# One cast and one subtraction per streamed weight tile instead of two of each

## The chip, the cores and the metric

The program runs on one core of a Trainium2 chip. The metric is the time of one execution on the device in microseconds (us), taken as the median of the runs; lower is better. Before the change the three runs took 1419.07, 1419.39 and 1425.46 us, so the median is 1419.39 us.

## The reference

The kernel computes one layer of a diffusion backbone for 256 latent tokens and 256 context tokens of width 2048, all in float32. Cut to what matters here:

```python
mod = silu(c) @ w_ada + b_ada                  # 2048 x 12288, six vectors
h  = rms_norm(x,   g_attn) * (1 + sc_a) + sh_a
hc = rms_norm(ctx, g_attn) * (1 + csc_a) + csh_a
q, k, v, ... = split(h @ w_in), split(hc @ w_in)   # 2048 x 4928
o = concat(neighbourhood(...), gqa(...), mla(...), diff(...))
x = x + gt_a * (o @ w_out)                     # 2048 x 2048
h = rms_norm(x, g_ffn) * (1 + sc_f) + sh_f
x = x + gt_f * ((silu(h @ wg) * (h @ wu)) @ wd)    # three of 2048 x 5632
return rms_norm(x, g_final)
```

Each weight matrix is read from DRAM once, a tile at a time.

## The kernel before, in words

TensorE multiplies in a rounded float32 form (F32R in the code). To keep the precision, every operand is split into a high part, which is the value cast to that form, and a low part, which is the value less the high part. A product is then three matmuls: high with high, high with low and low with high.

A streamed weight tile is 256 rows by 512 columns (320 or 256 in two places), that is two blocks k of 128 rows side by side in SBUF, `raw` [128, 2, 512]. Its way is always the same. SyncE (SP) issues one DMA of 512 KB into one of four `raw` buffers (`stream_raw`, L115). ScalarE (ACT) casts it into `whi`, one cast for each k (L127). VectorE (DVE) subtracts it into `wlo`, one subtraction for each k (L130). TensorE (PE) then runs the high products of both k (L150 and L151) and after them the low products (L153), in `mm3s`. `whi` and `wlo` have six buffers of [128, 512] each (`WB = 6`), enough for three weight tiles. A `raw` buffer comes free when the second subtraction has read it, and only then does SP issue the next DMA into it. The same four `raw` buffers also take the tiles of `w_ada` for the gate and FFN modulation vectors; those are multiplied and summed on DVE (`ada_block`, L335 on ACT for the first, L337 on DVE for the others), and they mingle with the weight tiles in two stretches of the run.

The stages in order of time are: tokens, normalisation and the first columns of the modulation (to about 60 us); the columns of `w_in` for the first two head groups, summed over five groups of K, with more of the modulation on TensorE (60 to 280); the other columns of `w_in` with the attention of the head groups in between (280 to 520); `w_out` (520 to 645); SwiGLU with `ffn_wg`, `ffn_wu` and `ffn_wd` (from 645), where `w_ada` tiles are still mixed in until about 820; and the final norm (from about 1400).

Two things set the order of the work. `Side` is a planner in the program's text: attention and modulation tasks are generators with costs in us, and `pump` traces their next stage between the weight tiles. What it decides does not depend on the split. Behind it the framework that builds the program lays the traced instructions out on each engine by the time at which it plans them to be ready, so the order on an engine is not quite that of the text; `tc.issue_after` (in `after`, with `newest`) pins a few instructions behind others. At run time each engine takes its instructions strictly in order.

Three more places keep split weights for longer, in pools of their own: `keep_w` (pool `rt`, `RT = 14` buffers, for the end of `w_out` and the first columns of `ffn_wg`), and the last columns of `ffn_wd` (pool `rt2`, 8 buffers). `stream_up` splits the small matrices of the latent attention, in one case as four blocks of 256 columns.

Of the kernel before, what the change touches and what calls it, by code (L numbers as in the profile page):

```python
# [10 lines left out]
F32 = mybir.dt.float32  # L11
F32R = mybir.dt.float32r
# [19 lines left out]
class Side:  # L32
    """Instructions traced in between the weight tiles of the main stream.

    A task is a generator that yields (time it takes of the tensor engine, time its
    results need) in us; its next stage is traced once the main stream has gone on
    for that long. Lanes are worked on independently, `width` tasks of a lane at once.
    """

# [48 lines left out]
def hybrid_dit_kernel(ctx: ExitStack, tc: tile.TileContext, a, out):  # L88
# [16 lines left out]

    # ------------------------------------------------------------ helpers
    def misc():
# [9 lines left out]

    WB = 6
    newest = {}

    def split(raw, n, keep=None):
        """hi and lo parts of raw [128, k, n], one pair per k"""
        out_ = []
        pool_, bufs = keep or (stream, WB)
        for k in range(raw.shape[1]):
            hi = pool_.tile([P, n], F32R, name="whi", tag="whi", bufs=bufs)
            act.copy(hi, raw[:, k])  # L127
            newest["act"] = nc.cur_bb.bb.instructions[-1]
            lo = pool_.tile([P, n], F32R, name="wlo", tag="wlo", bufs=bufs)
            dve.tensor_tensor(out=lo, in0=raw[:, k], in1=hi.bitcast(F32), op=ALU.subtract)  # L130
            newest["dve"] = nc.cur_bb.bb.instructions[-1]
            out_.append((hi, lo))
        return out_

# [4 lines left out]
    def after(*ins):  # L139
        """what the block traces on an engine of ins is issued behind them"""  # L140
        st = ExitStack()
        for i in ins:
            st.enter_context(tc.issue_after(i))
        return st

    def mm3s(jobs, w_left=False):
        """l @ r from their parts for each (bank, l, r, start, stop); the products with the
        low part of the weights come after all the others"""
        for dst, l, r, start, stop in jobs:
            pe.matmul(dst, lhsT=l[0], rhs=r[0], start=start, stop=False)  # L150
            pe.matmul(dst, lhsT=l[0 if w_left else 1], rhs=r[1 if w_left else 0], start=False, stop=False)  # L151
        for dst, l, r, start, stop in jobs:
            pe.matmul(dst, lhsT=l[1 if w_left else 0], rhs=r[0 if w_left else 1], start=False, stop=stop)  # L153
# [13 lines left out]

    # ------------------------------------------------------------ tokens and small vectors
    x_t = {}
# [43 lines left out]

    # ------------------------------------------------------------ normalised tokens, features on partitions
    xnT = [None] * 8
# [34 lines left out]
    def ada_pe(pr):  # L250
        """shift and scale of chunks 2 pr, 2 pr + 1 for both streams: column tile j of the
        tensor engine takes chunk j % 2 of the shift (j < 2) or the scale"""
        mv = misc()
        for k2 in range(0, KC, 2):
            raw = sb0.tile([P, 2, 2, 256], F32, name="araw", tag="araw", bufs=4)
            for kk in range(2):
                sp.dma_start(raw[:, kk], ada_two[:, k2 + kk, :, pr * 256:(pr + 1) * 256])
            for kk in range(2):
                kc = k2 + kk
                for j in range(4):  # L260
                    pe.matmul(mv[32 * j:32 * j + 32, :P], lhsT=cs32[:, kc, :], rhs=raw[:, kk, j // 2, tsl(j % 2)], start=(kc == 0), stop=(kc == KC - 1), skip_group_check=True)  # L261
            yield 0.5, 1.3
        mvs = sb0.tile([P, P], F32, name="mvs", bufs=2)
        act.copy(mvs, mv[:, :P])
        yield 0.0, 0.5
        cp = misc()
        pe.transpose(cp[:, :P], mvs, ident)
        cpv = cp[:, :P].rearrange("p (s j t) -> p s j t", s=2, j=2)[:, :, :, 0:2]
        k2 = slice(2 * pr, 2 * pr + 2)

        def col(c):
            return c.unsqueeze(2).to_broadcast([P, 2, 2])

        dve.tensor_tensor(out=scg[:, k2, :], in0=cpv[:, 1], in1=col(colA1[:, 16 + 2 * pr:18 + 2 * pr]), op=ALU.add)
        dve.tensor_tensor(out=scg[:, k2, :], in0=scg[:, k2, :], in1=col(colB[:, k2]), op=ALU.mult)
        dve.tensor_tensor(out=sha[:, k2, :], in0=cpv[:, 0], in1=col(colA[:, k2]), op=ALU.add)
        yield 0.1, 0.0
# [35 lines left out]

    # ------------------------------------------------------------ NA and GQA columns: summed over groups of K chunks on SBUF
    na_qT = kv.tile([P, 4, S], F32, name="qT", bufs=3)
# [5 lines left out]

    # ---- second use of w_ada: gate and FFN columns
    mcol = {s: const.tile([P, KC], F32, name=f"mcol{s}") for s in (2, 3, 4, 5)}
# [39 lines left out]
    def block(c0, prs, first, units):  # L363
        """one block of 512 columns over the K chunks of prs; a unit is (matmul operands, where its bank is added)"""
        accs = [acc() for _ in units]
        for pr in prs:
            w = stream_w(w_in, 2 * pr, c0, 512)
            for i, (form, where) in enumerate(units):
                mm3s([form(accs[i], w, 2 * pr + kk, pr == prs[0] and kk == 0, pr == prs[-1] and kk == 1) for kk in range(2)], c0 == NA_K)
                if pr == prs[-1]:  # L370
                    for dst, src in where(accs[i]):
                        add_up(dst, src, first)
                side.pump(1.3, 2.0)
# [35 lines left out]
    def prepare():  # L409
        """rope tables with the GQA gains in them, the NA bias with its mask, lambda"""  # L410
        xa = sb0.tile([P, 2, 4, S], F32, name="xa", tag="x_t", bufs=2)
# [85 lines left out]

    # ------------------------------------------------------------ the four head groups
    p_at = ExitStack()
# [22 lines left out]
    def proj(c0, n, toks, evac, hook=None):  # L522
        """columns c0.. of the input projection for token tiles toks; evac(t, psum) is a task"""
        accs = [acc() for _ in toks]
# [26 lines left out]
    def rope(dst, src, ct, st, nh, hd):  # L551
        """dst = src * ct + swap(src) * st over nh heads of width hd; ct, st [128, hd]"""
        half = hd // 2
# [9 lines left out]
    def soft(score, bias=None):  # L563
        """exp(score - max) of a [128, 512] score tile, and the reciprocal of its sum"""
        if bias is not None:
            dve.tensor_tensor(out=score[:, 0:S], in0=score[:, 0:S], in1=bias, op=ALU.add)
        st = small.tile([P, 4], F32, name="st")
        dve.tensor_reduce(out=st[:, 0:1], in_=score, axis=AX.X, op=ALU.max, negate=True)
        p = at.tile([P, 512], F32, name="p", bufs=3)
        act.activation(p, score, AF.Exp, bias=st[:, 0:1], accum_out=st[:, 1:2])  # L570
        dve.reciprocal(st[:, 2:3], st[:, 1:2])
        return p, st[:, 2:3]
# [37 lines left out]
    def gate_rows(seg, pool_):  # L610
        """the gate of seg as one row on all partitions, by way of DRAM"""
        ps = misc()
# [17 lines left out]

    # ---- grouped-query attention
    def head_rstd(ps, nh):
# [53 lines left out]

    # ---- multi-head latent attention
    c64, s64 = table("rope_c64", 64), table("rope_s64", 64)
# [109 lines left out]

    # ---- differential attention
    def dk_evac(t, ps):  # L800
# [63 lines left out]

    # ------------------------------------------------------------ output projection and residual
    side.finish(*gate_tasks)
# [49 lines left out]
    rt = p_rt.enter_context(tc.tile_pool(name="rt", bufs=1))  # L916
    RT = 14
    kept = [0]
# [44 lines left out]

    # ------------------------------------------------------------ SwiGLU
    def gu_jobs(ps, w_, k2, t):
# [91 lines left out]

    # ------------------------------------------------------------ the last columns one token tile after the other, final norm
    p_h2.close()
    rt2 = po.enter_context(tc.tile_pool(name="rt2", bufs=1, side="right"))  # L1060
    steps = [(fb, j) for fb in range(f0, f1) for j in (0, 2)]
    for t in range(2):
        for c0, cn in (((0, 512),) if t == 0 else ((0, 256), (256, 256))):
            ps = acc()
            for n, (fb, j) in enumerate(steps):
                if t == 0:
                    w_keep[fb, j] = stream_w(a["ffn_wd"], fb * 4 + j, 3 * 512, 512, (rt2, 8) if n < 4 else None)
                mm3s([(ps[:, :cn], sub(aT[fb], slice(None), j + kk, tsl(t)), sub(w_keep[fb, j][kk], slice(None), slice(c0, c0 + cn)), n == 0 and kk == 0, n == len(steps) - 1 and kk == 1) for kk in range(2)])
# [80 lines left out]
```

## Time and profile before

| | |
|---|---|
| three runs | 1419.07, 1419.39, 1425.46 us |
| profiled execution, first to last instruction (its span) | 1415.0 us |
| median of the runs less that span | 4.4 us |
| mean granted TensorE clock over the span | 0.996 of full speed |
| PE busy | 1375.5 us (97%) |
| DVE busy | 914.9 us (65%), of it the 764 subtractions L130 491.2 us |
| ACT busy | 618.9 us (44%), of it the 764 casts L127 433.0 us |
| read from DRAM | 310.36 MB |

The profile is of one execution, and of that execution only the span is known, not what the device spends before its first and after its last instruction. The median of the timed runs lies 4.4 us above the span. "Busy" is time in which an engine executes; an engine that waits for a semaphore or for a buffer is idle. An instruction's duration runs to the moment when its result is written, and the next one on ACT or DVE starts a little before that, so the durations of neighbours overlap.

### The profile page before, as it was taken

Reading aid. Unit: us, or ns where it says so; the run is one execution under the profiler, and the core shown is the slowest. Engines: PE = TensorE matmul, PEld = TensorE weight load, DVE = VectorE, ACT = ScalarE, POOL = GpSimd, SP = SyncE. Lnnn points to the kernel's source line nnn. Section 1 sums busy time; section 2 is a strip of 40 time slices with the busy share of each in tenths; the row PEclk is TensorE's granted clock in tenths of the full one; section 3 lists DMA queues with packets and bytes.
Section 4 is the critical chain, followed back from the end, with each engine's and each line's share of the span. In section 5 each row is a group of like instructions: output and inputs, shape, how many; then the busy total and the mean of one; then the engine's idle time right before and its main releaser. Section 6 shows DMA issues by size and latency. Waiting matters only on the chain.

```text
span 1415.0 us, 19888 instructions
## 1 busy us (share of the span) xinstructions
PE 1375.5 (97%) x7082; PEld 1082.3 (76%) x7082; DVE 914.9 (65%) x1623; ACT 618.9 (44%) x1180; POOL 34.1 (2%) x46
## 2 busy tenths in 40 slices
PE   6999999998999999999999999999999999999997
PEld 4766778766876687777877788888888888888886
DVE  3565679988888728779677854445545565555465
ACT  3522223464333525557444454444444443444443
POOL 1020000100000000000000000000000000000000
PEclk9999999999999999999999999999999999999999
DMA  9998896668879726356888876666666556666653
GB/s 324 322 318 278 282 312 215 205 215 264 270 246 298 230 90 235 124 175 188 290 272 281 293 239 194 185 190 180 191 182 183 182 182 196 183 188 181 185 167 139
DMA packets 183607, 313.78 MB, mean 222 GB/s; under 512 B 14002, under 2 KB 53972, under 8 KB 182356
## 3 DMA queue, kind: packets, MB, share of 16 engines
q1 hardware_dynamic: 179104, 302.03, 66.9%
q0 software_dynamic: 1056, 7.36, 1.3%
q10 hardware_dynamic: 3348, 3.13, 0.7%
q8 instruction: 55, 0.90, 0.3%
q14 instruction: 44, 0.36, 0.1%
HBM read 310.36 MB, written 2.11 MB: 221 GB/s over the span
## 4 chain that ended last, share of the span: by engine, by line
PE 74%; DMA 12%; DVE 8%; ACT 2%; issue 2%; POOL 0%; SPq 0%; ACTq 0%; POOLq 0%; DVEq 0%
PE acc L150 23%; PE acc L151 22%; PE acc L153 22%; DMA raw<-in_w_ada_dram 7%; DVE ada_acc L337 3%; DMA raw<-in_w_in_dram 3%; PE m L261 3%; DVE wlo L130 2%; DMA raw<-in_ffn_wg_dram 1%; ACT whi L127 1%; PE m L830 1%; DMA raw<-in_ffn_wu_dram 1%; DMA rowsB<-in_rows_dram 1%; PE m L232 1%; PE m L541 1%
## 5 line engine op out<-in xcount | busy, mean ns | idle before, releaser
L130 DVE TENSOR_TENSOR wlo<-raw,whi 128x512 fp32r<-128x512 f32 (+1 forms) x764 | 491.2, 682 | 354.0 <-ACT whi L127 345.8
L127 ACT CAST whi<-raw 128x512 fp32r<-128x512 f32 (+1 forms) x764 | 433.0, 614 | 618.6 <-PE acc L151 414.1
L150 PE MATMUL acc<-whi,h_hi 128*128 128x512 f32 x704 | 280.7, 399 | 2.5 <-ACT whi L127 2.5
L151 PE MATMUL acc<-whi,h_lo 128*128 128x512 f32 x704 | 279.1, 396 | 0.0
L153 PE MATMUL acc<-wlo,h_hi 128*128 128x512 f32 x704 | 195.7, 397 | 0.2 <-DVE wlo L130 0.2
L337 DVE SCALAR_TENSOR_TENSOR ada_acc<-raw,cs,ada_acc 128x512 f32<-128x512 f32 x210 | 157.1, 748 | 38.0 <-DMA raw<-in_w_ada_dram 28.7
L150 PE MATMUL acc<-whi,h 128*128 128x512 f32 (+1 forms) x416 | 166.8, 403 | 5.3 <-ACT whi L127 3.4
L150 PEld LDWEIGHTS acc<-whi,h_hi 128*128 128x128 f32 x704 | 132.6, 188 | 36.3 <-ACT whi L127 5.1
L151 PE MATMUL acc<-whi,h 128*128 128x512 f32 (+1 forms) x416 | 157.8, 381 | 0.0
L153 PEld LDWEIGHTS acc<-wlo,h_hi 128*128 128x128 f32 x704 | 132.6, 188 | 32.8 <-DVE wlo L130 0.7
L151 PEld LDWEIGHTS acc<-whi,h_lo 128*128 128x128 f32 x704 | 132.6, 188 | 31.4
L150 PE MATMUL acc<-whi,ah 128*128 128x512 f32 (+1 forms) x364 | 141.3, 390 | 0.0
L151 PE MATMUL acc<-whi,al 128*128 128x512 f32 (+1 forms) x364 | 140.9, 389 | 0.0
L153 PE MATMUL acc<-wlo,h 128*128 128x512 f32 (+1 forms) x416 | 114.4, 379 | 0.2 <-DVE wlo L130 0.2
L150 PEld LDWEIGHTS acc<-whi,h 128*128 128x128 f32 x416 | 78.3, 188 | 30.5 <-issue 11.0
L153 PE MATMUL acc<-wlo,ah 128*128 128x512 f32 (+1 forms) x364 | 98.7, 389 | 0.0
L153 PEld LDWEIGHTS acc<-wlo,h 128*128 128x128 f32 x416 | 76.0, 188 | 15.7 <-DVE wlo L130 1.4
L151 PEld LDWEIGHTS acc<-whi,h 128*128 128x128 f32 x416 | 78.4, 188 | 12.5 <-issue 1.2
L150 PEld LDWEIGHTS acc<-whi,ah 128*128 128x128 f32 x364 | 68.6, 188 | 15.5
L151 PEld LDWEIGHTS acc<-whi,al 128*128 128x128 f32 x364 | 68.6, 188 | 15.4
L153 PEld LDWEIGHTS acc<-wlo,ah 128*128 128x128 f32 x364 | 67.7, 188 | 15.6
L150 PE MATMUL acc<-whi,o_hi 128*128 128x512 f32 x128 | 51.8, 406 | 0.0
(228 smaller groups left out, 1278.6 us busy)
## 6 DMA issues: line engine op xcount, KB each, us to landing
raw<-in_w_ada_dram SPq DMA_DIRECT2D x112, 512.0 KB, 4.6
raw<-in_ffn_wg_dram SPq DMA_DIRECT2D x88, 512.0 KB, 3.8
raw<-in_ffn_wu_dram SPq DMA_DIRECT2D x88, 512.0 KB, 3.9
raw<-in_ffn_wd_dram SPq DMA_DIRECT2D x88, 512.0 KB, 4.6
raw<-in_w_in_dram SPq DMA_DIRECT2D x72, 512.0 KB, 5.0
araw<-in_w_ada_dram SPq DMA_DIRECT2D x128, 256.0 KB, 4.8
raw<-in_w_out_dram SPq DMA_DIRECT2D x32, 512.0 KB, 3.9
araw<-in_w_ada_dram SPq DMA_DIRECT2D x16, 512.0 KB, 5.7
```

The costliest lines, as they stand in the source:

```text
L127: act.copy(hi, raw[:, k])
L130: dve.tensor_tensor(out=lo, in0=raw[:, k], in1=hi.bitcast(F32), op=ALU.subtract)
L150: pe.matmul(dst, lhsT=l[0], rhs=r[0], start=start, stop=False)
L151: pe.matmul(dst, lhsT=l[0 if w_left else 1], rhs=r[1 if w_left else 0], start=False, stop=False)
L153: pe.matmul(dst, lhsT=l[1 if w_left else 0], rhs=r[0 if w_left else 1], start=False, stop=stop)
L232: pe.transpose(ps[:, kk * S + t * P:kk * S + (t + 1) * P], x_t[2 * w + t][:, tsl(2 * pr + kk)], ident)
L261: pe.matmul(mv[32 * j:32 * j + 32, :P], lhsT=cs32[:, kc, :], rhs=raw[:, kk, j // 2, tsl(j % 2)], start=(kc == 0), stop=(kc == KC - 1), ski ...
L337: dve.scalar_tensor_tensor(out=acc_, in0=raw[:, kk, :], scalar=cs[:, 0, kc:kc + 1], in1=acc_, op0=ALU.mult, op1=ALU.add)
L541: pe.transpose(ps[:, tsl(j)], src[:, tsl(j)], ident)
L830: pe.matmul(sc, lhsT=df_qT[hb, h, tsl(t)], rhs=df_kT[h // 2][hb, h % 2, :], start=True, stop=True)
```

## The change

`split` makes one cast and one subtraction over the whole tile [128, k, n]; the pieces for each k are views of it. The number of buffers is halved where each is twice as large, so the bytes are the same: `WB` from 6 to 3, `RT` from 14 to 7, and 8 to 4 for the last columns of `ffn_wd`. The remaining lines of the diff are comments and docstrings that are emptied. No DMA, no matmul and no use of `after` is changed; `newest` now points at the merged instructions.

```diff
-    WB = 6
+    WB = 3
...
     def split(raw, n, keep=None):
         pool_, bufs = keep or (stream, WB)
-        for k in range(raw.shape[1]):
-            hi = pool_.tile([P, n], F32R, name="whi", tag="whi", bufs=bufs)
-            act.copy(hi, raw[:, k])
-            newest["act"] = nc.cur_bb.bb.instructions[-1]
-            lo = pool_.tile([P, n], F32R, name="wlo", tag="wlo", bufs=bufs)
-            dve.tensor_tensor(out=lo, in0=raw[:, k], in1=hi.bitcast(F32), op=ALU.subtract)
-            newest["dve"] = nc.cur_bb.bb.instructions[-1]
-            out_.append((hi, lo))
-        return out_
+        nk = raw.shape[1]
+        hi = pool_.tile([P, nk, n], F32R, name="whi", tag="whi", bufs=bufs)
+        act.copy(hi, raw)
+        newest["act"] = nc.cur_bb.bb.instructions[-1]
+        lo = pool_.tile([P, nk, n], F32R, name="wlo", tag="wlo", bufs=bufs)
+        dve.tensor_tensor(out=lo, in0=raw, in1=hi.bitcast(F32), op=ALU.subtract)
+        newest["dve"] = nc.cur_bb.bb.instructions[-1]
+        return [(hi[:, k], lo[:, k]) for k in range(nk)]
...
-    RT = 14
+    RT = 7
...
-                    w_keep[fb, j] = stream_w(a["ffn_wd"], fb * 4 + j, 3 * 512, 512, (rt2, 8) if n < 4 else None)
+                    w_keep[fb, j] = stream_w(a["ffn_wd"], fb * 4 + j, 3 * 512, 512, (rt2, 4) if n < 4 else None)
```

## Rows read from the trace of the kernel before

**Rows 1.** The page's first part: busy time of each engine over the span.

```profile
span 1415.0 us, 19888 instructions
PE 1375.5 (97%) x7082; PEld 1082.3 (76%) x7082; DVE 914.9 (65%) x1623; ACT 618.9 (44%) x1180; POOL 34.1 (2%) x46
```

**Rows 2.** Stretches: length, busy us of PE, PEld, DVE, ACT, POOL, clock, DMA.

```profile
60.00:280.00 220.00, 220.00 (x1651) 166.08 (x1650) 164.51 (x331) 70.83 (x132) 15.03 (x13) 1.00 0.84 271
280.00:480.00 200.00, 187.34 (x924) 144.79 (x923) 169.26 (x321) 89.19 (x203) 6.08 (x7) 1.00 0.79 255
...
690.00:820.00 130.00, 127.54 (x562) 101.14 (x561) 97.42 (x154) 56.66 (x102) 0.00 (x0) 1.00 0.83 278
820.00:1400.00 580.00, 580.00 (x2524) 467.85 (x2523) 309.69 (x488) 256.71 (x461) 1.06 (x2) 1.00 0.61 186
```

**Rows 3.** Groups by shape: busy us, mean ns of one, idle before them.

```profile
L130 DVE TENSOR_TENSOR wlo<-raw,whi 128x512 fp32r<-128x512 f32 x744 | 482.5, 687 | 351.7 <-ACT whi L127 345.8 <-PE acc L153 4.3 <-PE acc L151 0.8
L127 ACT CAST whi<-raw 128x512 fp32r<-128x512 f32 x744 | 425.1, 618 | 602.5 <-PE acc L151 414.1 <-DMA raw<-in_w_in_dram 59.4 <-DMA raw<-in_ffn_wg_dram 38.5
...
L130 DVE TENSOR_TENSOR wlo<-raw,whi 128x256 fp32r<-128x256 f32 x4 | 1.4, 420 | 2.2 <-PE m L153 2.2
...
L127 ACT CAST whi<-raw 128x256 fp32r<-128x256 f32 x4 | 1.3, 402 | 0.8 <-PE m L151 0.8
```

**Rows 4.** Timeline, saturated stage: start, us from first start to last end.

```profile
899.44 1.29 DVE L130 TENSOR_TENSOR wlo<-raw,whi 128x512 fp32r<-128x512 f32 x2 [1.51 <-ACT whi L127]
...
901.02 1.14 ACT L127 CAST whi<-raw 128x512 fp32r<-128x512 f32 x2 [1.67 <-PE acc L151]
```

**Rows 5.** Waits of ACT from 820 to 1390: us, times, longest.

```profile
ACT whi L127 <- PE acc L151: 305.8, 195, 1.7
```

**Rows 6.** Timeline, one stall of PE at 759 us.

```profile
758.84 1.14 ACT L127 CAST whi<-raw 128x512 fp32r<-128x512 f32 x2 [3.68 <-DMA raw<-in_ffn_wg_dram]
759.49 1.29 DVE L130 TENSOR_TENSOR wlo<-raw,whi 128x512 fp32r<-128x512 f32 x2 [0.91 <-ACT whi L127]
...
759.51 0.51 PE L150 MATMUL acc<-whi,h_hi 128*128 128x512 f32 x1 [1.01 <-ACT whi L127]
...
760.09 0.45 PE L150 MATMUL acc<-whi,h_hi 128*128 128x512 f32 x1
```

**Rows 7.** Waits of PE and of its weight loads, whole run.

```profile
PE acc L150 <- ACT whi L127: 5.9, 6, 1.8
...
PE acc L153 <- DVE wlo L130: 1.2, 3, 0.8
...
PEld acc L150 <- ACT whi L127: 11.9, 22, 2.2
...
PEld acc L153 <- DVE wlo L130: 5.1, 13, 1.1
```

**Rows 8.** Chain of waits, 755 to 769 us: start, us, what.

```profile
755.84 1.30 DVE wlo L130 x2
...
757.15 4.81 DMA raw<-in_w_ada_dram
...
762.73 1.30 DVE wlo L130 x2
...
764.04 4.51 DMA raw<-in_ffn_wu_dram
```

**Rows 9.** Waits of DVE, first row 280 to 480, second 690 to 820.

```profile
DVE wlo L130 <- ACT whi L127: 8.9, 10, 3.6
...
DVE wlo L130 <- ACT whi L127: 15.9, 16, 2.8
```

**Rows 10.** Subtractions in these stretches: length, busy us of PE, PEld, DVE.

```profile
280.00:480.00 200.00, 52.24 (x216) 37.30 (x216) 41.44 (x70) 1.00 0.79 255
...
690.00:820.00 130.00, 47.95 (x176) 32.64 (x174) 54.98 (x85) 1.00 0.83 278
```

**Rows 11.** Timeline, the first weight tile.

```profile
26.07 0.62 ACT L127 CAST whi<-raw 128x512 fp32r<-128x512 f32 x1 [2.62 <-DMA raw<-in_w_in_dram]
26.60 0.61 ACT L290 CAST h<-h_f 128x512 fp32r<-128x512 f32 x1
...
27.26 0.80 PE L150 MATMUL acc<-h,whi 128*128 128x256 f32 x2 [3.43 <-ACT h L290]
```

More of the change, by code (lines that the diff above doesn't have):

```diff
@@ L116, in stream_raw @@
         return raw
-    WB = 6
+    WB = 3
     newest = {}
     def split(raw, n, keep=None):
-        out_ = []
         pool_, bufs = keep or (stream, WB)
-        for k in range(raw.shape[1]):
-            hi = pool_.tile([P, n], F32R, name="whi", tag="whi", bufs=bufs)
-            act.copy(hi, raw[:, k])
-            newest["act"] = nc.cur_bb.bb.instructions[-1]
-            lo = pool_.tile([P, n], F32R, name="wlo", tag="wlo", bufs=bufs)
-            dve.tensor_tensor(out=lo, in0=raw[:, k], in1=hi.bitcast(F32), op=ALU.subtract)
-            newest["dve"] = nc.cur_bb.bb.instructions[-1]
-            out_.append((hi, lo))
-        return out_
+        nk = raw.shape[1]
[6 more added lines that the diff above has]
+        return [(hi[:, k], lo[:, k]) for k in range(nk)]
     def stream_w(w, k0, c0, n, keep=None):
```

## The prediction

> **What bounds the kernel now.** I read the page's busy times first, then the stretches, then who waits for whom, and last the chain of waits and the timeline at the places where TensorE stands still. PE is busy for 1375.5 of 1415.0 us [rows 1], so at most 39.5 us can be won by feeding it better. The stretches say where those lie [rows 2]. From 60 to 280 and from 820 to 1400 us PE is busy all the time: 800 us of the span in which no faster cast or subtraction can help, and in which a later one costs nothing as long as PE finds its next weight tile ready. From 280 to 480 PE lacks 12.7 us (200.00 less 187.34), from 690 to 820 it lacks 2.5 us. The rest, 24.3 us, lies in the start to 60 us, in 480 to 690 and in the end after 1400.
>
> In the full stage the casts are not late but early: from 820 to 1390 ACT waited 195 times for PE to release a `whi` buffer, 305.8 us in all, 1.57 us each time [rows 5]. Elsewhere PE does wait for the split. It stood still 6 times for a cast, 5.9 us, and 3 times for a subtraction, 1.2 us; its weight loads were held up 22 and 13 times, 11.9 and 5.1 us [rows 7]. Why the split is late there is shown by the chain of waits around 755 to 769 us [rows 8]: two subtractions end at 757.14, at 757.15 the DMA into the freed `raw` buffer is issued, it takes 4.81 us, and at 762.73 the next subtractions follow; they end at 764.03, and at 764.04 the next DMA goes out. One turn of this ring is 6.9 us, and the subtraction that ends last is a link of it.
>
> **The change part by part.** The trace of before has no cast of 2x512 columns, so its price is bounded. A cast of 512 columns takes 618 ns and one of 256 takes 402 ns [rows 3], 0.84 ns a column; a subtraction takes 687 and 420 ns, 1.04 ns a column. By these slopes 1024 columns take 618 + 512 x 0.84 = 1.05 us on ACT and 687 + 512 x 1.04 = 1.22 us on DVE. From below they are bounded by one piece (0.62 and 0.69 us), from above by the two pieces as they run today one behind the other, 1.14 and 1.29 us from the first start to the last end [rows 4]. I take the slopes, which lie near the upper end. So a tile saves only 0.09 us of ACT and 0.07 us of DVE, not the sum of two fixed costs, because neighbours already overlap. Over some 380 tiles that is 34 and 27 us of engines that are busy 44% and 65% of the span; almost all of it falls where they wait for PE anyway.
>
> What it moves. The first `whi` is ready 1.05 us after the cast starts, not 0.62; the second 1.05, not 1.14. The first `wlo` comes much later, and the second, where DVE has been idle, at 1.05 + 0.03 + 1.22 = 2.30 us instead of 1.94 (759.49 + 1.29 less 758.84 [rows 6]), 0.36 later. Where DVE has work queued and the cast is long done, the last `wlo` comes 0.07 earlier.
>
> *Buffers.* A pair is now released in one piece, when PE has done the high products of both k. In the jobs of SwiGLU the second k ends two matmuls after the first, and a matmul takes 580.00/2524 = 0.23 us [rows 2], so the cast may start 0.46 us later. It is cast for a use three tiles on, so this is hidden by two tiles of 12 matmuls, 5.5 us; if that cover were gone it would cost 0.46 + 0.43 us a tile. From 60 to 280 and from 820 to 1400 I cost the change at 0. Behind the waiting cast on ACT stand copies from PSUM; they start at most 0.4 us later, and there are four accumulators for two in use.
>
> *PE waits for a cast.* At 758.84 the cast starts, at 759.51 comes the first matmul, and the third, the first with the second k, comes at 760.09, 1.25 us after the cast's start [rows 6]. With one cast the first comes at 1.05 + 0.05 = 1.10 and the third two matmuls later, at 1.56: 0.31 us later than today. The low products follow after eight high ones, at 2.9 us, and find `wlo` ready at 2.30. Six such stalls [rows 7] make +1.9 us; were all 22 held weight loads such stalls, 6.8 us. I take 1.9.
>
> The Trainium skill has a rule that speaks against this change: its page "Perfetto Trace Analysis", section "Optimizing Scalar/DVE Operations", says that larger operations help a saturated engine, but that where ScalarE and VectorE are not saturated and yet leave gaps on another engine, breaking instructions up lets work be done sooner. DVE's 169.26 of 200 and 97.42 of 130 us in the two starved stretches are not saturation, so by the rule merging loses wherever PE waits, all 22 times; by the row on PE itself it loses six times.
>
> *PE waits for a subtraction.* Two low products of a pair then follow one end instead of the second following its own: one matmul more, 0.23, less 0.07 us, is 0.16. Three times [rows 7] make +0.5 us; 13 times 2.1.
>
> *The ring.* The two starved stretches are 330 us, 48 turns of 6.9 us. Weight tiles share the buffers with `w_ada` tiles, so I take half the turns, 24, as going by a subtraction. In these stretches there are 70 and 85 subtractions [rows 10], about 78 pairs, and DVE waited for the cast 26 times [rows 9]. So a third of the releases come 0.36 later and two thirds 0.07 earlier: 24 x (0.12 - 0.05) = +1.7 us. The bounds are 24 x 0.36 = +8.6 and 24 x -0.07 = -1.7 us.
>
> *The start.* The first cast runs at 26.07, the cast of the tokens behind it at 26.60, the first matmul at 27.26 [rows 11]. One cast of 1.05 us pushes the token cast to 27.07 and PE to 27.7: +0.4 us. If the token cast is put ahead, PE starts at 27.2: -0.1 us. I take +0.4.
>
> *Relief of DVE among the attention tasks.* 35 pairs from 280 to 480 x 0.07 = 2.5 us less DVE work, in a stretch where softmax and rope steps queue on DVE behind subtractions. It can be worth 0 to -2.5 us; I take -1.0, since 85% of DVE's time is taken there.
>
> The sum is 0.4 + 1.9 + 0.5 + 1.7 - 1.0 = +3.5 us. On the profiled execution this makes a span of 1418.5 us; the median of the runs lies 4.4 us above the span, and I leave that as it is: 1423 us, 0.25% more.
>
> **The rivals.**
>
> *Faster by relief.* Larger instructions could cost less than the slopes say, or the freed time could take the attention stalls away. For it: PE lacks 12.7 us from 280 to 480, where DVE is 85% busy [rows 2]. Against it: the saving is 2.5 us of DVE there. If half of what PE lacks in both starved stretches went, 7.6 us, the time would be 1412 us.
>
> *Slower by the ring.* If in the starved stretches the cast, not DVE's queue, is what the subtraction waits for, each release comes 0.36 late: +8.6 us, and with PE's waits at their upper ends (6.8 and 2.1) and the start's 0.4 it makes 17.9 us, 1437 us. The rule on breaking up work, cited above, expects this sign. It decides from the point at which more than about half of the pairs find DVE idle; today it is a third [rows 9]. At half the pairs it is +3.5 from the ring, and about 1425 us.
>
> *Another order.* The first weight cast ran before the token cast although the text has it behind [rows 11], so the engines' order is planned by expected times, and instructions twice as long can be placed otherwise among rope, softmax and `w_ada` steps. The longest waits that PE itself has for a cast are 1.8 us [rows 7]; four such waits more or less are 7 us to either side: 1416 or 1430 us. Nothing in the profile says which sign.
>
> *No change at all.* PE's work is the same and the stretches without waits hold 800 us; if new and old delays fall into waits for DMA, the time stays at 1419 us.
>
> **How the numbers follow.** I give the forecast with its near neighbour, no change, 0.56; relief 0.14; the ring 0.18; another order 0.12, as likely early as late. This measurement can tell about 0.5% from no change, that is 7.1 us: 1412.3 and 1426.5 are the borders. The forecast's own bounds, 1419 to 1428, lie mostly inside, with 0.07 of its chance above the upper border. Half of the relief, 0.07, lies below the lower one; of the ring 0.16 lies above the upper one; of another order 0.03 lies below and 0.05 above. So faster 0.10, slower 0.28, and the same 0.62. The range is 1411 to 1434: below it lie the deeper reliefs, above it the ring at full price.
>
> **What would show it.** In the profile after, 382 or so casts of about 1.05 us and subtractions of about 1.22 us; their busy sums on ACT and DVE down to about 400 and 465 us. PE full as before from 60 to 280 and 820 to 1400. Around PE's stalls the first matmul about 1.1 us after the cast's start, not 0.67. More PE idle time from 690 to 820. The prediction is wrong if PE gets gaps in the full stages, which would mean that the three buffers no longer hold enough; if the merged instructions take clearly less or more than the slopes; or if PE's idle time from 280 to 480 moves by more than 5 us, which would speak for another order.

## The result, and the profile after

The changed kernel takes 1434.0 us in the median (1430.79 to 1436.61, four runs), beside 1419.72 us for the kernel before in the same session. The ratio is 1.0099, 95% interval 1.0076 to 1.0121: 14 us slower. That is more than the 0.5% that the prediction named as the least that can be told, and the time stands at the upper edge of the predicted range. The profiled execution has a span of 1428.7 us, against 1415.0. Both profiles are of quick executions: the changed kernel's took 1430.79 us, the shortest of its four and 2.1 us above its span, so by the same difference (an estimate) the one profiled before took about 1417 us, and about half of the 4.4 us between span and median before is that execution's own speed.

The first part of the page of the kernel after, and its two groups of the split (line, operation, count, busy us, mean ns, idle before):

```profile
span 1428.7 us, 18526 instructions
...
PE 1380.1 (97%) x7082; PEld 1086.6 (76%) x7082; DVE 888.5 (62%) x1240; ACT 584.3 (41%) x797; POOL 35.8 (3%) x46
...
L129 DVE TENSOR_TENSOR wlo<-raw,whi 128x1024 fp32r<-128x1024 f32 (+1 forms) x381 | 462.5, 1216 | 373.2 <-ACT whi L126 370.6
L126 ACT CAST whi<-raw 128x1024 fp32r<-128x1024 f32 (+1 forms) x381 | 397.0, 1044 | 654.2 <-PE acc L149 474.0
```

DVE and ACT have 26 and 35 us less to do than in [rows 1], and PE, with the same matmuls, is busy 4.6 us longer. The stretches of the kernel after, in the columns of [rows 2] (length; busy us of PE, PEld, DVE, ACT, POOL; granted clock; DMA share; GB/s), with two shorter ones:

```profile
60.00:280.00 220.00, 220.00 (x1660) 167.73 (x1659) 161.92 (x295) 68.35 (x95) 14.73 (x13) 1.00 0.84 273
280.00:480.00 200.00, 186.29 (x912) 147.23 (x910) 162.70 (x277) 81.50 (x157) 6.70 (x7) 0.97 0.80 253
690.00:820.00 130.00, 127.39 (x558) 100.85 (x557) 95.27 (x111) 51.09 (x56) 0.00 (x0) 1.00 0.84 276
820.00:1400.00 580.00, 580.00 (x2514) 467.28 (x2513) 294.80 (x279) 239.67 (x255) 1.05 (x2) 1.00 0.63 190
440.00:500.00 60.00, 55.59 (x221) 36.28 (x221) 44.83 (x74) 25.59 (x53) 0.00 (x0) 0.97 0.71 226
620.00:690.00 70.00, 63.02 (x274) 48.79 (x273) 52.88 (x79) 40.94 (x69) 3.38 (x3) 0.98 0.61 195
```

The two shorter ones in the kernel before:

```profile
440.00:500.00 60.00, 58.88 (x246) 39.91 (x245) 45.33 (x81) 26.80 (x59) 0.00 (x0) 1.00 0.75 240
620.00:690.00 70.00, 68.56 (x303) 53.28 (x302) 60.60 (x110) 47.17 (x96) 1.99 (x3) 1.00 0.69 226
```

The full stages are as full as before. Most of what is lost lies in the two short stretches: PE's busy time there is 3.3 and 5.5 us less. The same is seen by following a landmark: the time at which a group of matmuls first or last runs. The latent attention's scores begin 0.5 us later than before (449.2 for 448.7 us) and end 6.4 later (485.6 for 479.2); the first matmul with `h_hi` is 8.1 later (653.8 for 645.7); the first with `ah` 13.8 (850.4 for 836.6), and so is the last (1419.5 for 1405.7). Behind 850 us nothing more is lost.

At the first place, VectorE's timeline of the kernel before (start, us, what, count, idle before it):

```profile
449.75 4.69 DVE L337 SCALAR_TENSOR_TENSOR ada_acc<-raw,cs,ada_acc 128x512 f32<-128x512 f32 x6 [0.83 <-DMA raw<-in_w_ada_dram]
454.36 0.68 DVE L568 TENSOR_REDUCE st<-m 128x1 f32<-128x512 f32 x1
```

and of the kernel after, with ScalarE's cast a little later:

```profile
450.15 7.05 DVE L335 SCALAR_TENSOR_TENSOR ada_acc<-raw,cs,ada_acc 128x512 f32<-128x512 f32 x9 [1.52 <-DMA raw<-in_w_ada_dram]
457.12 0.68 DVE L566 TENSOR_REDUCE st<-m 128x1 f32<-128x512 f32 x1
...
467.72 1.04 ACT L126 CAST whi<-raw 128x1024 fp32r<-128x1024 f32 x1 [2.88 <-DMA raw<-in_w_in_dram]
468.67 1.07 ACT L803 COPY tok<-acc 128x512 f32<-128x512 f32 x2
469.63 1.09 ACT L542 COPY pT<-m 128x512 f32<-128x512 f32 x2
```

No instruction of the split stands in the first two rows. Three more steps of the modulation stand ahead of the softmax's maximum, which so comes 2.76 us later. Then a cast that waits for its DMA stands ahead of four copies from PSUM, of which PE waits for the last two (`pT`, 0.72 us); before, these copies had gone first, at 463.93 to 466.00, and the casts at 471.39. PE has five stalls here, ending between 460.80 and 470.28 us, of 0.7 to 1.2 us each; before it had two in the same work, of 0.69 and 0.43 us.

At the second place the norm ahead of SwiGLU is late. ScalarE of the kernel before:

```profile
653.22 1.34 ACT L932 ACTIVATE xn<-x,rstd 128x512 f32<-128x512 f32 x2 [1.44 <-POOL rstd L162]
...
664.00 1.13 ACT L947 CAST h_hi<-hf 128x512 fp32r<-128x512 f32 x2
```

ScalarE of the kernel after, and the matmul that waits:

```profile
662.42 1.06 ACT L126 CAST whi<-raw 128x1024 fp32r<-128x1024 f32 x1 [1.71 <-DMA raw<-in_ffn_wu_dram]
664.53 1.34 ACT L930 ACTIVATE xn<-x,rstd 128x512 f32<-128x512 f32 x2 [1.05 <-POOL rstd L160]
...
667.39 1.05 ACT L126 CAST whi<-raw 128x1024 fp32r<-128x1024 f32 x1 [0.91 <-DMA raw<-in_ffn_wu_dram]
668.34 0.80 ACT L942 ACTIVATE hf<-m,mcol,mcol 128x128 f32<-128x128 f32 x2
...
671.42 0.73 PE L148 MATMUL acc<-whi,h_hi 128*128 128x512 f32 x2 [3.44 <-ACT h_hi L945]
```

The first matmul with `h_hi` came 8.1 us later than before; `xn` of the second tile of tokens (the 256 latent tokens are two tiles of 128) came 11.3 later. Its next step, `hf`, stands behind a cast for the up-projection, a tile that PE uses only behind the 48 gate matmuls of these tokens (16 blocks k of three products; 48 x 0.23 = 11 us), and that cast waits for a DMA.

Some of the loss is not idle time at all. The granted clock of the kernel after in stretches around 351, 472 and 674 us (length, PE busy and matmuls, clock, DMA share, GB/s):

```profile
351.00:354.40 3.40, 3.00 (x11) 0.53 0.81 271
...
471.00:474.00 3.00, 3.00 (x9) 0.50 0.78 257
474.00:477.00 3.00, 3.00 (x18) 0.99 0.97 328
...
672.50:675.50 3.00, 3.00 (x9) 0.51 0.68 234
```

For some 3.4 us at a time the clock is at its lower level, 1.2 GHz; PE is "busy" and does half as many matmuls. There are four such stretches between PE's start-up and the end (the fourth at 385.5); the profile of the kernel before has none there. Half of 3.4 us, 1.7, is lost in each, 6.8 us in all. The two ahead of 425 us are made up for by then, since the landmark there, the first matmul with `ckvT`, is only 0.3 us late: from 280 to 425 us PE stands idle 2.2 us less than before. So of the 13.7 us by which the spans differ at most the other two falls, 3.4 us, are the clock's.

### The profile page after: what moved, and what is told of

It is laid out like the page before. It is cut to its first block, busy times and chain, and to the rows that moved or that the text cites. A ratio compares the mean times of both kernels' runs of the same rounds, so it can differ in the third digit from the quotient of the medians.

```text
span 1428.7 us, 18526 instructions
## 1 busy us (share of the span) xinstructions
PE 1380.1 (97%) x7082; PEld 1086.6 (76%) x7082; DVE 888.5 (62%) x1240; ACT 584.3 (41%) x797; POOL 35.8 (3%) x46
## 4 chain that ended last, share of the span: by engine, by line
PE 77%; DMA 11%; DVE 7%; ACT 2%; issue 2%; POOL 0%; ACTq 0%; POOLq 0%; DVEq 0%; SPq 0%
PE acc L148 24%; PE acc L149 23%; PE acc L151 22%; DMA raw<-in_w_ada_dram 5%; DVE ada_acc L335 3%; DMA raw<-in_w_in_dram 3%; PE m L259 3%; DVE wlo L129 2%; ACT whi L126 2%; PE m L590 1%; DMA araw<-in_w_ada_dram 1%; PE m L539 1%; DMA raw<-in_ffn_wg_dram 1%; PE m L230 1%; DMA raw<-in_ffn_wu_dram 1%
## 5 line engine op out<-in xcount | busy, mean ns | idle before, releaser
L129 DVE TENSOR_TENSOR wlo<-raw,whi 128x1024 fp32r<-128x1024 f32 (+1 forms) x381 | 462.5, 1216 | 373.2 <-ACT whi L126 370.6
L126 ACT CAST whi<-raw 128x1024 fp32r<-128x1024 f32 (+1 forms) x381 | 397.0, 1044 | 654.2 <-PE acc L149 474.0
```

What stands on the lines that cost most here:

```text
L126: act.copy(hi, raw)
L129: dve.tensor_tensor(out=lo, in0=raw, in1=hi.bitcast(F32), op=ALU.subtract)
```

## The experiments

Theory A: the longer instructions made the framework lay out another order of the other work, and it is the order that costs the time. Rivals: B, the lengths themselves; C, the buffers that are now released in pairs. In the built programs the order has indeed moved: 64 of VectorE's 861 instructions that don't belong to the split, and 16 of ScalarE's 369, stand elsewhere.

The two profiles show that it is not these two engines alone. Compared by tile names, TensorE's own matmuls stand in another order at some 50 places, and so do some of SyncE's DMA issues between 43 and 137 us: no matmul and no DMA was changed, but their order was. At the second place, for instance, TensorE transposes `xn` in three goes before, and in two after (first the kernel before):

```profile
640.18 1.09 PE L939 MATMUL m<-ident,xn 128*128 128x128 f32 x8
642.04 0.60 PE L939 MATMUL m<-ident,xn 128*128 128x128 f32 x4
643.87 0.60 PE L939 MATMUL m<-ident,xn 128*128 128x128 f32 x4
```

```profile
648.83 1.53 PE L937 MATMUL m<-ident,xn 128*128 128x128 f32 x12
651.12 0.60 PE L937 MATMUL m<-ident,xn 128*128 128x128 f32 x4
```

The swaps below move the order of all engines at once, and the profiles bear this out: with before's order, the matmuls and the DMA issues follow each other as in the kernel before throughout. Whose order costs the time no run takes apart.

The kernels that take over an order are built twice. The first pass only yields the order that the framework lays out for one form of the split; in the second pass every instruction of an engine is chained behind its neighbour of that order, whatever its length, and the waits for data stay as they are. The edit, cut to what matters:

```diff
+            if order:
+                for e, row in order.items():        # one row for each engine
+                    last = None
+                    for x in spread(row, made):
+                        if last is not None:
+                            tc.add_manual_dep(x, last.name, ...NoSync...)
+                        last = x
...
+    order = build(ORDER)[1] if ORDER else None
+    nc = build(FORM, order)[0]
```

Each ratio is against the kernel before in the same session, where its median was 1416.06 to 1418.89 us; it is not the quotient of the two medians and can lie some 0.1% off it. The interval behind it is one of 95%.

**Short instructions in the order of the changed kernel** (pair buffers, two casts, two subtractions).

> Two casts and two subtractions for each weight tile again, in pair buffers, but every engine is made to issue its instructions in the order that the changed kernel's program has; the two pieces stand one behind the other where the whole one stood. Theory A, the order in which the plan puts the engines' other work is what costs: the time stays with the changed kernel, 1428 to 1437 us, with PE idle about 460 to 485 us and at 650 to 675 us. Theory B, the longer instructions themselves cost (later first piece, later release of the raw buffer): it comes back to 1417 to 1423 us. Theory C, that a pair of buffers is released in one piece: 1428 to 1437 us, as in A.

Measured: 1428.99 us, ratio 1.0094 (1.0077 to 1.0112). Without one long instruction nearly the whole loss is there. PE's stall ahead of the second tile's `h_hi` is there too, 2.86 us. In this profile the second place costs more than in the changed kernel, 198.1 us from the first `h_hi` to the first `ah` for 190.9 before (196.6 there), and the first place less: the scores are 1.1 us late at their start and 3.6 at their end.

**Long instructions in the order of the kernel before.**

> One cast and one subtraction of 2x512 columns as in the changed kernel, but every engine issues in the order that the program of before has; the whole operation stands where its first piece stood. Theory A, order: 1416 to 1424 us, with the two stalls of the changed kernel gone. Theory B, length: 1428 to 1437 us. Theory C, pair buffers: 1428 to 1437 us. My prediction's terms for the length alone (later first cast, ring) would give 1420 to 1424 us.

Measured: 1419.26 us, ratio 1.0027 (1.0005 to 1.0049). The stretches of this kernel (length, PE, clock, DMA share, GB/s):

```profile
280.00:480.00 200.00, 188.68 (x929) 1.00 0.79 256
...
440.00:500.00 60.00, 58.35 (x242) 1.00 0.72 237
620.00:690.00 70.00, 67.59 (x300) 1.00 0.68 223
690.00:820.00 130.00, 126.82 (x557) 1.00 0.82 277
```

Both short stretches are back within 1 us of before, no clock falls, and the first `h_hi` matmul runs at 645.7 us as before. With long instructions the order is worth 1.0099 less 1.0027, 0.72% or 10.2 us; with short ones 0.94%, 13.3 us. The lengths and buffers are worth 0.27% (3.8 us, by its interval 0.7 to 7.0) in the one order and 0.05% in the other, which can't be told from zero. Each ratio is uncertain by some 0.2%, so these differences are by some 0.3%. The kernel before, chained in its own order, was not run; what the chaining itself costs is counted in the 0.27%.

**Pair buffers alone**, with the order that the framework makes for them.

```diff
-            hi = pool_.tile([P, n], F32R, ..., bufs=6)
+        hi = pool_.tile([P, nk, n], F32R, ..., bufs=3)   # two casts, two subtractions on hi[:, k]
```

> Only the buffers are changed: three of [128, 2, 512] instead of six of [128, 512], two casts and two subtractions as before, order as planned for this program. Theory A: near before, 1415 to 1426 us, as far as its planned order differs little from that of before. Theory B: 1417 to 1422 us. Theory C: 1428 to 1437 us.

Measured: 1419.85 us, ratio 1.0014 (0.9991 to 1.0036). Rival C falls as the cause of the 14 us. The order of this kernel differs from before's too, at fewer places (25 of VectorE's other instructions in the profiles), and costs nothing that can be told.

**Half of the order.** The long form again; chained as in the kernel before is only what is traced ahead of the output projection (first run), or only what is traced from there on (second run).

```diff
+                if n in part:              # n < cut, or n >= cut
+                    bound.add(x.name)
-                    for x in spread(row, made):
+                    for x in (x for x in spread(row, made) if x.name in bound):
```

> The changed kernel with its long casts and subtractions; every engine's order is that of the kernel before for all that is traced ahead of the output projection (the projections, the four attention groups), and the planner's own behind it. Of the 861 other VectorE instructions 12 then stand elsewhere than before, all behind the projection, where the changed kernel has 64; of ScalarE's 369 4 where it has 16. Theory A (the planned order of the other work, in two separate places): the 6.4 us lost at 449 to 485 us come back, the 7.4 us lost at 636 to 675 us stay; 1427 to 1428 us, ratio 1.005 to 1.007, h_hi first at 646 to 647 us and the first ah at 844 to 845. Rival B (what goes wrong at 636 to 675 us only follows from what came late at 449 to 485): the order ahead is enough, 1419 to 1421 us, ratio 1.002 to 1.004. Rival C (the early part's order is not at fault, the loss lies in the lengths): 1432 to 1434 us.

Measured: 1425.83 us, ratio 1.0049 (1.0033 to 1.0066). The first `h_hi` matmul is back at 647.6 us; from there to the first `ah` it takes 195.2 us, 4.2 more than before.

> The same with the parts exchanged: the planner's own order up to the output projection, the order of the kernel before from there on. Theory A: the 6.4 us at 449 to 485 us stay, the 7.4 us at 636 to 675 us come back; 1426 to 1428 us, ratio 1.005 to 1.007, h_hi first at 652 to 654 us, the first ah 192 us later (as before). Rival B: what is late at 485 us carries the norm's steps with it and nothing comes back, 1432 to 1434 us. Rival C: 1432 to 1434 us too, told from B by the run with the early part's order.

Measured: 1424.32 us, ratio 1.0042 (1.0024 to 1.0060). The first `h_hi` matmul is late, at 653.1 us, and from there to the first `ah` it takes 190.8 us, as before (190.9). The stretches of the first of these kernels and then of the second:

```profile
440.00:500.00 60.00, 57.47 (x237) 1.00 0.71 235
620.00:690.00 70.00, 63.96 (x278) 0.98 0.60 198
```

```profile
440.00:500.00 60.00, 56.93 (x228) 0.97 0.71 233
620.00:690.00 70.00, 68.01 (x301) 1.00 0.64 211
```

In these profiles each half of the order brings back its own place and leaves the other. These are two losses, each about half, and the second is not a consequence of the first. (The two gains, 0.50 and 0.57%, add up to more than the 0.72% of the whole order; the intervals are too wide to tell this from chance.)

**Half of the split**, each with the order that the framework makes for it: one cast and two subtractions, then two casts and one subtraction.

```diff
-            act.copy(hi[:, 0], raw[:, 0]); act.copy(hi[:, 1], raw[:, 1])
+            act.copy(hi, raw)
```

> Half of the change alone, with the planner's own order: one cast of 2x512 columns, two subtractions of 512, tiles of twice the size. By the lengths alone 1.2 to 1.9 us over the kernel before (the waits for a cast), less the share of the subtractions. Theory A: any change of a length makes another order, of either sign: 39 of 861 VectorE instructions and 19 of 369 of ScalarE's stand elsewhere, and on the chip it lies anywhere from 1416 to 1434 us, its loss or gain at the places where the order differs (a run of subtractions, accumulations or casts ahead of a softmax or norm step), not spread over the stages where TensorE is full. Rival (the long cast itself costs the 14 us): 1430 us or more with stalls of TensorE that end in a wait for a cast.

Measured: 1426.45 us, ratio 1.0060 (1.0035 to 1.0084).

> The other half alone: two casts of 512 columns, one subtraction of 2x512. By the lengths alone 0.5 us of waits less 1.0 us of VectorE's relief: 1416 to 1418 us in the call's kernel before of 1417 to 1419. Theory A: another order again (70 of 861 VectorE instructions, 19 of 369 of ScalarE's), 1416 to 1434 us, with what is lost or won at the places where the order differs. Rival (the long subtraction costs the 14 us): 1430 us or more, with TensorE's stalls ended by waits for a subtraction.

Measured: 1425.31 us, ratio 1.0039 (1.0024 to 1.0054). Neither half reaches the 1430 us of its rival, and both are slower than the sum of their lengths. Theory A's own range, 1416 to 1434 us, was so wide that these two hardly test it. No order that the framework made for another form of the split was faster: +0.99, +0.14 (which can't be told from zero), +0.60 and +0.39%.

**A remedy for the second place**, tried on the changed kernel, on it with before's order in the early part, and on the kernel before.

```diff
-            w_ = stream_w(w, k2, fb * 512, 512)
+            with after(*(normed.values() if fb == 0 else ())):   # the norm's last cast and subtraction
+                w_ = stream_w(w, k2, fb * 512, 512)
```

> The changed kernel with one thing told to the planner: the casts and subtractions of the first up-projection's weight tiles are issued behind the norm's last cast and subtraction on their engines. All else is the planner's. If the late half of the loss (5.7 us from the first h_hi matmul to the first ah, on top of the 190.9 us of before) comes from weight casts that stand ahead of the norm's steps and wait for their DMA, the stretch falls from 196.6 to between 191 and 193 us and the stall of 3.60 us ahead of the first h_hi matmuls of token tile 1 to under 1 us: 1428 to 1430 us, ratio 1.005 to 1.008. If the casts only happened to stand there and the norm is late by its own chain (xn, transposes, hf), the stall stays and the time is 1432 to 1435 us. If the pinned casts now come too late for the up-projection, TensorE stalls for a cast at some 680 us, and the stretch is 196 us or more again.

Measured: 1430.34 us, ratio 1.0089 (1.0064 to 1.0114). ScalarE and the waiting matmul of this kernel:

```profile
664.38 1.34 ACT L932 ACTIVATE xn<-x,rstd 128x512 f32<-128x512 f32 x2 [3.82 <-POOL rstd L160]
...
667.47 1.77 ACT L944 ACTIVATE hf<-m,mcol,mcol 128x128 f32<-128x128 f32 x4 [1.14 <-DVE hf L946]
669.14 1.13 ACT L947 CAST h_hi<-hf 128x512 fp32r<-128x512 f32 x2
```

The cast ahead of `hf` is gone and PE's stall falls from 3.44 to 1.99 us. But ScalarE now stands idle for 3.82 us ahead of `xn`, which comes no earlier: it waits for the norm's own chain on VectorE and GpSimd. Further on, between 751 and 818 us, PE has six stalls of 0.4 to 0.7 us for the split (3.3 us), where the changed kernel had four (2.5 us); whether they come from the tiles that are held back is not shown. From the first `h_hi` to the first `ah` it takes 195.7 us, 1 us less. I expected 191 to 193 and a ratio of 1.005 to 1.008; that was wrong.

> The run with before's order ahead of the output projection (ratio 1.0049), and the same pin for the first up-projection's casts and subtractions behind the norm. If both places are then mended, nothing is left but the lengths: ratio 1.001 to 1.0035, 1420 to 1424 us, the first h_hi matmul at 646 to 648 us and the first ah 191 to 193 us later (195.2 in the run without the pin). If the pin does not take back the late part, 1.0045 to 1.006.

Measured: 1427.13 us, ratio 1.0069 (1.0051 to 1.0088). Expected were 1.001 to 1.0035 if the pin mended the second place. It did not; whether it is worse than without the pin (1.0049, 1.0033 to 1.0066) is not told.

> The kernel before with the same pin; its order changes by one ScalarE instruction (the cast of one up-projection tile goes behind the norm's last h_hi). There the stretch has stalls of 0.2 to 0.4 us only, so at most 1 us is to be had: ratio 0.9985 to 1.001. If the pin delays the up-projection's tiles it shows here alone, as a stall for a cast at some 670 us and a ratio above 1.002.

Measured: 1418.35 us, ratio 0.9991 (0.9967 to 1.0015): no difference, as expected. So the pin wins no time that these runs can tell: the cast that was seen ahead of `hf` lengthens PE's stall, by 1.45 us between the two profiles, but by itself it is not the cause of the second place.

**Half of the split in the order of the kernel before.** These two were to give the terms of my sum one by one; the order is chained as in the second experiment.

> One cast of 2x512 columns, still two subtractions of 512, all engines in the order of the kernel before. My sum gives this half the waits for a cast (+1.9), the start (+0.4) and what the ring loses to a later first release: +2 to +4 us, ratio 1.0015 to 1.003. With the planner's own order the same instructions gave 1.006. If the order is the cause of the rest, it is below 1.004 here; if the long cast is, it stays at 1.006.

Measured: 1428.04 us, ratio 1.0080 (1.0060 to 1.0100).

> Two casts of 512 columns, one subtraction of 2x512, all engines in the order of the kernel before. My sum gives this half the waits for a subtraction (+0.5) less the relief of VectorE (-1.0), and a share of the ring: -1 to +1.5 us, ratio 0.999 to 1.001. With the planner's own order it was 1.0039. If the order is the cause of that, it is below 1.002 here; if the long subtraction is, 1.003 or more.

Measured: 1426.14 us, ratio 1.0065 (1.0046 to 1.0084). Both came out on the side that I had put down for the lengths: in an order that doesn't move, one long instruction costs more (0.80 and 0.65%) than both together (0.27%). In its profile (an execution of 1431.34 us) the first loses at yet another place: the first matmul with `ckvT` is 7.7 us later than before already (432.8 us). VectorE and TensorE of the kernel with the long cast alone:

```profile
385.58 1.29 DVE L151 TENSOR_TENSOR wlo<-raw,whi 128x512 fp32r<-128x512 f32 x2 [2.76 <-ACT whi L144]
...
388.51 0.15 DVE L379 TENSOR_TENSOR mcol<-mcol,colA 128x4 f32<-128x4 f32 x1
...
388.74 0.66 PE L574 MATMUL m<-ident,tok 128*128 128x128 f32 x2 [4.18 <-DVE mcol L379]
```

The same in the kernel with both long:

```profile
378.15 1.23 DVE L153 TENSOR_TENSOR wlo<-raw,whi 128x1024 fp32r<-128x1024 f32 x1 [0.85 <-ACT whi L143]
...
381.01 0.15 DVE L378 TENSOR_TENSOR mcol<-mcol,colA 128x4 f32<-128x4 f32 x1
...
381.24 0.41 PE L573 MATMUL m<-ident,tok 128*128 128x128 f32 x2 [1.65 <-DVE mcol L378]
```

The order is the same: a subtraction, and behind it the modulation step for which PE waits. In the first kernel the cast of that subtraction's tile came later, and the wait grew from 0.85 to 2.76 us on VectorE, from 1.65 to 4.18 on PE. The stretch from 340 to 400 us of the kernel with the long cast alone, then of the one with both long:

```profile
340.00:400.00 60.00, 50.35 (x283) 0.94 0.72 233
```

```profile
340.00:400.00 60.00, 55.30 (x339) 1.00 0.81 259
```

So theory A holds as far as its runs reach: of the loss of the changed kernel most goes with its order, whatever the lengths. It doesn't hold as the rule that an order has a price of its own. Before's order is good with the two lengths of before and nearly as good with two long instructions, and bad with one of each kind. Why one long instruction is worse there than two stays open: these are single profiles, and no run takes the DMA's landing apart from the order. The stall shown is 2.5 us longer, which is not the whole of the 7.7.

## Why the prediction was right or wrong

*Prices of the instructions: right.* A merged subtraction takes 1225 ns and a merged cast 1051 ns (predicted 1.22 and 1.05 us); the busy sums are 462.5 and 397.0 us (465 and 400).

*The full stages: right.* 220.00 and 580.00 us of PE.

*PE waits for a cast: right at the stall, wrong in the sum.* ScalarE and TensorE of the kernel after, at a stall that ends in a cast:

```profile
752.96 1.98 ACT L126 CAST whi<-raw 128x1024 fp32r<-128x1024 f32 x2
...
754.04 0.50 PE L148 MATMUL acc<-whi,h_hi 128*128 128x512 f32 x1 [0.85 <-ACT whi L126]
...
754.61 0.40 PE L148 MATMUL acc<-whi,h_hi 128*128 128x512 f32 x1
```

The first matmul comes 1.08 us after the cast's start (1.10), the first with the second k after 1.65 (1.56). But PE's waits for a cast did not grow. In the kernel after, and with long instructions in before's order (us, times, longest):

```profile
PE acc L148 <- ACT whi L126: 5.3, 7, 1.4
```

```profile
PE acc L182 <- ACT whi L143: 4.5, 8, 1.5
```

Before they were 5.9 us in 6 [rows 7], so the +1.9 us is not there. PE's waits for a subtraction are 1.4 and 1.3 us, for 1.2: of the +0.5 at most 0.2. PE's idle time from 690 to 820 us, which was to grow, did so by 0.15 us, and in before's order by 0.72.

The rule of the Trainium skill, page "Perfetto Trace Analysis", section "Optimizing Scalar/DVE Operations", is that breaking work up may let it be done sooner where ScalarE and VectorE are not saturated and yet leave gaps on another engine. The time has the sign that merging would then have, by 0.27% in before's order; that it comes by such gaps the waits do not show, and 0.72% comes from elsewhere.

*The ring: the end was right, the comparison was not.* From a cast's start to the end of its last subtraction, worked out over all tiles from 690 to 820 us, the median is 2.35 us with long instructions in before's order (2.30 predicted), but 2.48 in the kernel before, where I had set 1.94 from one stall for a third of the tiles. Typical tiles are not released later, so +1.7 us had no ground.

*Relief of DVE: there.* From 280 to 480 us PE is busy 1.3 us longer with long instructions in before's order (188.68) than in [rows 2]; I had taken 1.0. In the changed kernel the gain is not there (186.29).

*The start: not told apart.* The first matmul runs at 26.9 us after the change, 0.4 earlier; with long instructions in before's order at 26.5.

*The sum: near in size, by luck.* +3.5 us predicted, +3.8 (0.7 to 7.0) measured in before's order. But its terms are not what makes it up: the waits for a cast and for a subtraction hardly moved, the ring's +1.7 had no ground, the start is not told apart, and the halves alone gave 0.80 and 0.65%, +11.4 and +9.2 us. Where the 3.8 us arise stays open. That 1434.0 us lies within 1411 to 1434 is luck too: the upper end stood for the ring at its full price, which did not come, and another order was priced up to 1430.

*The step that failed is "Another order".* I saw that the order is laid out by expected times and that longer instructions may change it. I priced it from four stalls at 7 us to either side, gave it 0.12, "as likely early as late", and left it out of the sum. It was the main term: +10.2 us, on top of the +3.8, never on the faster side in the orders tried, and in the profile partly by a road that I had not priced, the clock that falls behind the new stalls. The mark by which I wanted to know it failed as well: PE's idle time from 280 to 480 us was to move by more than 5 us. It moved by 1.05 (187.34 to 186.29 busy): half of the loss lies behind 480 us, and three of the four falls of the clock lie in this stretch, where matmuls at half the clock count as busy. What did show it is the count of matmuls and the clock of the same row, 912 at 0.97 for 924 at 1.00.

## What to carry to other kernels

Where a framework lays out the order by expected durations, changing the length of an instruction that occurs hundreds of times reorders work that has nothing to do with it, on every engine that it plans, here TensorE and the DMA queue too: compare the two orders first, and price the places where waiting instructions now stand ahead of what TensorE needs. To tell the order from the instruction, swap them: the old order with the new instructions and the new order with the old ones. Then test one step in between, since an order that suits two forms may still suit neither of their halves.

## What the runs showed of the hardware

The granted clock fell to its lower level, 1.2 GHz, for about 3.4 us behind stalls of PE (idle before, by the timeline): behind 0.75 and 1.66 us at 349.19 and 351.40, 3.08 at 384.03, 3.44 at 671.42, and the five stalls of 0.7 to 1.2 us between 460.80 and 470.28. In the kernel before, stalls of 1.83 and 1.57 us at 345.42 and 351.81 and of 1.87 at 382.06 were followed by no fall, so the length of one stall doesn't tell. A stall so can cost up to 1.7 us more than its own length, in a place where the busy share shows nothing.

Which falls there are differs from execution to execution: the kernel before with the pin, of the same time as before (0.9991), shows three in its profile, at 284.9, 465.9 and 773.0 us. Over the whole execution the changed kernel's mean granted clock was 0.988 to 0.991 in its four runs, that of the kernel before 0.993 to 0.997 in the 19 runs beside the first three experiments.
